# Two changes together in a two-block transformer kernel: squares summed on TensorE, and 17 weight residues prepared during block 1

## The chip, the cores and the metric

One core of one Trainium2 chip runs the whole program once. The metric is the device time of one execution in microseconds (us), the median of several runs.

## What is computed

The input x is 512 tokens by 1024 features, in fp32. It goes through two blocks, and the second takes the output of the first.

Block 1 is a mixer (chunk-band attention beside a multi-scale pooling path, joined by sigmoid gates) and a feed-forward part. In both places the result is normalised, added to x, and the sum is normalised again for the next projection:

```python
mix = (g_a * y_a + g_b * y_b) @ w_o[l]
x = x + rms_norm(mix, norm_mix_post[l])
f = conv_gated_ffn(rms_norm(x, norm_ffn_pre[l]), w_up[l], conv_w[l], conv_b[l], w_down[l])
x = x + rms_norm(f, norm_ffn_post[l])
```

Block 2 normalises x, projects it with w_in, and runs two branches on the projections: a gated delta rule (four heads, chunks of 64 tokens, a triangular solve for each chunk) and differential attention (four heads). Both results are normalised, gated and projected by w_out:

```python
hn = rms_norm_2(x, w_norm)
proj = jnp.einsum("bsd,de->bse", hn, w_in.astype(f32))
a_mat = lower + jnp.eye(c, dtype=q.dtype)
sol = lax.linalg.triangular_solve(a_mat, rhs, left_side=True, lower=True, unit_diagonal=True)
o = jnp.concatenate([o_a, o_b], axis=-1).astype(x.dtype)
return jnp.einsum("bse,ed->bsd", o, w_out)
```

## The kernel before, in words

**Layout.** Activations lie feature-major: the residual `xs` is 8 tiles of 128 features by 512 tokens. A weight piece is 128 output features by 1024 inputs (128x1024 fp32, 512 KB). `fetch` (line 371) loads pieces from DRAM on SyncE's queue into two raw buffers. `split_next` (line 382) cuts a piece into two fp32r operands: ScalarE copies it into `whi` (`split_hi`, line 350), VectorE subtracts that from the piece and writes the residue `wlo` (`split_lo`, line 356). There are four buffers of each. For every 128 inputs TensorE then does three matmuls: high by high, high by low, low by high.

**What sets the order.** The program is written out at build time by a planner, the class `Issue` (line 108). The main line issues matmuls; after each of them `step` (line 192) lets waiting generator tasks (`spawn`, line 189) issue their next instructions on the other engines, if the planner's own estimate of the engines' free times allows it. `after` (line 309) holds a task until its inputs are due, `room` (line 313) until VectorE and ScalarE have space. The order on each engine that comes out is fixed. Nearly all instructions of TensorE, VectorE, ScalarE and GpSimd come out of one helper, line 232, loads out of line 283, moves between on-chip memory and DRAM out of line 288.

**The seams.** Between a projection and the next one stands a norm, an addition and another norm. There are two such places, handled by the class `Seam` (line 518): after w_o (about 300 to 342 us) and after w_down (about 673 to 728 us). Tokens go in two halves of 256. `chain(hf)` (line 543) takes the column sums of squares of the projection's result (`rstd`, line 506: `colsum` on TensorE, one-column products `t<-ones,acc`; then a chain of 128x2 operations on VectorE, `ms`, `rsq_y`, `rsq_t`, `nc`; then `spread`, products `t<-cst,nc` that lay the factor over all partitions). For each of the 8 feature tiles it then computes on VectorE `f`, the addition into `x`, and the residue `nl`, and on ScalarE the high part `nh` and the square `sq`. GpSimd adds the squares of tiles 1 to 7 into `acc2`. After the last tile a second `rstd` on `acc2` gives the factor of the second norm, which goes into `nb` and multiplies the next projection's outputs. While this runs, TensorE does the products of the first four pieces of the next projection on each half as its tiles come out (`seam_products`, line 994: three products of 256 columns by four pieces for each tile; their tiles are `mm`, `s`, `s`, `t`). Behind the seam come units of 24 matmuls of 512 columns.

**Block 2.** Its input projection's pieces come in the order of `UNITS` (line 33). The delta rule works on two pairs of heads (`gdn_pair`, line 1165). For each pair VectorE and TensorE make the matrix L; it goes to DRAM (`dl<-L`), its diagonal blocks come back (`xt<-dl`), GpSimd solves them in about 14 us of small steps (`cb<-xt`, `xt<-xt,cb`), and the inverse goes out and comes back in its place (`dx<-xt`, `T<-dx`). TensorE then builds the full inverse (`s<-cst,T` and what follows). All these moves are on SyncE's queue, between the loads of weight pieces.

Of the kernel before, what the change touches and what calls it, by code (L numbers as in the profile page):

```python
# [17 lines left out]
P = 128  # L18
# [17 lines left out]
HEADS = [3, 0, 4, 2, 1, 5, 6, 7]  # L36
NHELD, NFIRST = 1, 6
NPART = 7
ATTN, DIFF = 6, 7
# [198 lines left out]
def kernel(ctx, tc, aps, out, dbg=None):  # L238
# [70 lines left out]
    def after(*aps):  # L309
        while iss.ready(*aps) > iss.now + LEAD:  # L310
            yield
# [49 lines left out]


    plan = weight_order()
    raws, done = [], []
# [17 lines left out]
    def split_next():  # L382
# [21 lines left out]
        else:  # L404
            off = (TOKOFF if n <= D else 0) if key[0] in tokmajor else HALFOFF if key[:2] in halves else 0
            hi = wbuf("whi", n, off)
            lo = wbuf("wlo", n, off)
            split_hi(raw, hi)
            yield
            split_lo(raw, hi, lo)  # L410
        done.append((key, hi, lo))
# [78 lines left out]

    def colsum(acc, tbs):
        ps = yield from grab("t")
        yield from after(acc[:, tbs[0] * P:(tbs[-1] + 1) * P])
        for i, tb in enumerate(tbs):
            T.matmul(ps[:, i:i + 1], acc[:, csl[tb]], ones, start=True, stop=True)
        yield
        return ps
# [20 lines left out]
    class Seam:  # L518
# [24 lines left out]
        def chain(self, hf):  # L543
# [3 lines left out]
            if hf == 0:  # L547
                self.col, self.col2, self.acc2, self.nb = tiny("nc", NT), tiny("nc", NT), act("acc"), act("nb")
            b = yield from rstd(self.acc, self.col, tbs)
            while hf and self.prog[0] < KD - 1:  # L550
                yield
            for k in range(KD + 1):
                if k < KD:
# [6 lines left out]
                    split_hi(x, self.hi[k][:, cs], pcol(self.gnext, k))  # L560
                    if k == 0:
                        A.activation(self.acc2[:, cs], x, AF.Square)
                    else:
                        sq = act("sq")
                        A.activation(sq[:, cs], x, AF.Square)
                        G.tensor_tensor(self.acc2[:, cs], self.acc2[:, cs], sq[:, cs], op=ALU.add)
                if k == KD - 1:
# [5 lines left out]
                yield from room()  # L573
            b = yield from rstd(self.acc2, self.col2, tbs)
            A.activation(self.nb[:, cs], b[:, :256], AF.Copy)
# [418 lines left out]
    def seam_products(sn, keys, finish):  # L994
# [16 lines left out]
        for hf in range(2):  # L1011
            for k in range(KD):
# [4 lines left out]
                if hf and k in (0, 4):  # L1017
# [5 lines left out]
    hhi, hlo, rb = seam_products(sn, [("w_up", i) for i, _ in units[:NS]],  # L1023
                                 lambda key, r: conv3(key[1] // 2 + key[1] % 2 * MF, r))
    for i, c in units[NS:]:
        w = weights("w_up", i)
        ps = grab_now("mm")
        gemm(ps, w, hhi, hlo)
        spawn(ffn_unit(c, ps, sn))
# [830 lines left out]
```

## Time and profile before

| | us |
|---|---|
| median of 3 runs | 1009.82 |
| lowest and highest run | 1008.95, 1013.06 |
| the profiled execution, its own time | 1010.56 |
| its span in the trace | 1008.8 |
| TensorE busy in it | 990.9 (98%) |
| VectorE busy | 682.7 (68%) |
| ScalarE busy | 497.7 (49%) |
| GpSimd busy | 83.6 (8%) |

The profiled execution's time is 1.76 us longer than its span (what lies before the first and behind the last instruction), and 0.74 us above the median. PE is TensorE's matmuls and PEld its weight loads, DVE is VectorE, ACT ScalarE, POOL GpSimd, SP SyncE; a q behind the name is that engine's DMA queue. Matmuls overlap, so the pace of TensorE is read from one start to the next and not from a single duration. One fp32 product is two instructions in the trace, one fp32r product is one.

### The profile page before, as it was taken

To read this page: it belongs to the slowest core of one execution; us is meant where nothing else is said; L and a number is where in the kernel's file an instruction comes from. 1 tells how busy PE (TensorE), PEld (TensorE's weight loads), DVE (VectorE), ACT (ScalarE), POOL (GpSimd) and SP (SyncE) were. 2 spreads that over 40 slices of the span, in tenths; PEclk is the share of its full clock that TensorE was granted. 3 is DMA by queue.
4 is the path that set the end of the run, shared out by engine and by line. 5 is a ranking of instruction groups with operands and counts; after the bars stand their busy time and mean duration, and the time that the engine had idled before them with its cause. 6 is when DMAs were issued, how large, how long until landed. Compare 5 with 4: busy or idle time off the path is not lost.

```text
span 1008.8 us, 14943 instructions
## 1 busy us (share of the span) xinstructions
PE 990.9 (98%) x5622; PEld 838.1 (83%) x5622; DVE 682.7 (68%) x1409; ACT 497.7 (49%) x1035; POOL 83.6 (8%) x162
## 2 busy tenths in 40 slices
PE   9999999999999999999999999999999998999998
PEld 7877688888898888888888888898899987888986
DVE  6587774444348997677677522259895687999973
ACT  6577533233354555344344422334456756578780
POOL 2010000000002100000001000003200261002001
PEclk9999999999999999999999999999999999999999
DMA  7422123232240132322323323230523441113322
GB/s 251 157 73 77 60 84 104 85 104 101 88 139 29 64 124 85 104 102 87 105 91 114 103 91 115 90 129 1 180 93 113 135 94 38 41 34 111 108 64 83
DMA packets 40344, 97.17 MB, mean 96 GB/s; under 512 B 12160, under 2 KB 16528, under 8 KB 40272
## 3 DMA queue, kind: packets, MB, share of 16 engines
q1 hardware_dynamic: 37392, 87.53, 26.6%
q0 software_dynamic: 2736, 8.66, 2.5%
q8 instruction: 44, 0.72, 0.3%
q14 instruction: 28, 0.23, 0.1%
q10 hardware_dynamic: 144, 0.03, 0.0%
HBM read 90.29 MB, written 5.91 MB: 95 GB/s over the span
## 4 chain that ended last, share of the span: by engine, by line
PE 82%; DVE 12%; DMA 2%; ACT 2%; issue 2%; SPq 0%; DVEq 0%; POOLq 0%; POOL 0%
PE mm L232 73%; PE t L232 6%; PE s L232 4%; DVE nl L232 2%; DVE x L232 2%; DVE wlo L232 1%; DVE f L232 1%; DVE y L232 1%; DMA w<-w_qk 1%; DVE rsq_t L232 1%; DVE acc L232 1%; DMA w<-w_a 0%; ACT whi L232 0%; DMA w<-w_v 0%; DVE r L232 0%
## 5 line engine op out<-in xcount | busy, mean ns | idle before, releaser
L232 DVE TENSOR_TENSOR wlo<-w,whi 128x1024 fp32r<-128x1024 f32 (+4 forms) x153 | 180.5, 1186 | 63.7 <-ACT whi L232 63.6
L232 PE MATMUL mm<-nh,whi 128*128 128x512 f32 x448 | 176.1, 393 | 0.3 <-DVE r L232 0.3
L232 PE MATMUL mm<-nl,whi 128*128 128x512 f32 x448 | 176.0, 393 | 0.0
L232 ACT ACTIVATE whi<-w 128x1024 fp32r<-128x1024 f32 (+4 forms) x153 | 155.0, 1018 | 42.3 <-DMA w<-w_dn 21.2
L232 PE MATMUL mm<-nh,wlo 128*128 128x512 f32 x448 | 175.8, 392 | 0.0
L232 PEld LDWEIGHTS mm<-nh,whi 128*128 128x128 f32 x448 | 84.2, 188 | 17.6 <-issue 0.7
L232 PEld LDWEIGHTS mm<-nh,wlo 128*128 128x128 f32 x448 | 84.1, 188 | 16.8
L232 PEld LDWEIGHTS mm<-nl,whi 128*128 128x128 f32 x448 | 84.2, 188 | 16.4
L232 PE MATMUL mm<-h,whi 128*128 128x512 f32 x208 | 82.4, 396 | 0.0
L232 PE MATMUL mm<-l,whi 128*128 128x512 f32 x208 | 82.1, 395 | 0.0
L232 PE MATMUL mm<-h,wlo 128*128 128x512 f32 x208 | 82.1, 395 | 0.0
L232 PE MATMUL mm<-gh,whi 128*128 128x512 f32 (+1 forms) x198 | 72.4, 366 | 0.0
L232 PE MATMUL mm<-gl,whi 128*128 128x512 f32 (+1 forms) x198 | 72.2, 365 | 0.0
L232 PE MATMUL mm<-gh,wlo 128*128 128x512 f32 (+1 forms) x198 | 72.2, 365 | 0.0
L232 ACT ACTIVATE y<-hu,par 128x512 f32<-128x512 f32 x40 | 32.4, 810 | 63.5 <-DVE hu L232 63.5
L232 DVE SCALAR_TENSOR_TENSOR y<-hu,par,y 128x511 f32<-128x511 f32 x80 | 59.9, 748 | 1.4
L232 POOL TENSOR_TENSOR acc<-acc,sq 128x256 f32<-128x256 f32 (+1 forms) x31 | 26.4, 851 | 413.8 <-ACT sq L232 413.7
L232 PE MATMUL mm<-wlo,nh 128*128 128x256 f32 (+1 forms) x192 | 54.7, 285 | 0.0
L232 PE MATMUL mm<-whi,nl 128*128 128x256 f32 (+1 forms) x192 | 54.6, 284 | 0.0
L232 DVE TENSOR_TENSOR hu<-mm,nb 128x512 f32<-128x512 f32 x40 | 27.6, 691 | 39.4 <-PE mm L232 39.4
L232 PE MATMUL mm<-whi,nh 128*128 128x256 f32 (+1 forms) x192 | 54.2, 282 | 0.0
L232 DVE TENSOR_TENSOR acc<-acc,sq 128x512 f32<-128x512 f32 (+1 forms) x21 | 14.3, 683 | 48.8 <-ACT sq L232 48.6
(352 smaller groups left out, 2166.3 us busy)
## 6 DMA issues: line engine op xcount, KB each, us to landing
w<-w_up SPq DMA_DIRECT2D x44, 512.0 KB, 3.5
w<-w_g SPq DMA_DIRECT2D x16, 512.0 KB, 3.5
w<-w_dn SPq DMA_DIRECT2D x16, 448.0 KB, 3.4
w<-w_a SPq DMA_DIRECT2D x12, 512.0 KB, 3.5
w<-w_ap SPq DMA_DIRECT2D x8, 512.0 KB, 3.5
w<-w_o SPq DMA_DIRECT2D x8, 512.0 KB, 3.4
w<-w_dn SPq DMA_DIRECT2D x8, 512.0 KB, 3.5
w<-w_z SPq DMA_DIRECT2D x8, 512.0 KB, 3.6
```

What stands on the lines that cost most here:

```text
L232: return f(*args, **kw)
```

## The change

Two edits.

**Squares.** `acc2` and its GpSimd additions are gone. ScalarE writes the squares of the 8 tiles into 8 tiles of their own (`sqs`), and `colsum` takes the list: for each block of 128 tokens it sums all 8 tiles in PSUM, 16 one-column products for each half where there were 2.

**Residues ahead.** A new task, `make_ahead`, runs during block 1's up projection, for 17 pieces of block 2: q0 (two pieces), k0 (two), k1 (two), v1 (two), the eight of z, and a11. It loads each piece in two halves of 128x512 on GpSimd's queue, ScalarE makes the high part, VectorE the residue, and GpSimd's queue stores the residue in DRAM (`low_...`). In block 2 `split_next` then loads the stored residue into `wlo` on SyncE's queue in place of VectorE's subtraction. `whi` is made as before.

```diff
@@ -35,6 +35,8 @@
 
 HEADS = [3, 0, 4, 2, 1, 5, 6, 7]
 NHELD, NFIRST = 1, 6
+
+AHEAD = ["q0", "k0", "k1", "v1"]
 NPART = 7
 ATTN, DIFF = 6, 7
 START = [("w", 0, 0), ("x", 0, 0), ("x", 1, 0), ("w", 1, 0), ("x", 2, 0), ("x", 3, 0),
@@ -360,6 +362,29 @@
             V.scalar_tensor_tensor(lo, src, scale, hi.bitcast(F32), op0=ALU.mult, op1=ALU.subtract)
 
 
+    made = {}
+
+    def make_ahead(keys):
+        for key in keys:
+            src = aps[key[0]][key[1]]
+            parts = [slice(0, 512), slice(512, src.shape[-1])]
+            low = dp.tile([P, src.shape[-1]], F32, name=f"low_{key[0]}_{key[1]}")
+            raw = [act("pr") for _ in parts]
+            for t, sl in zip(raw, parts):
+                load(nc.gpsimd, t, src[:, sl])
+            yield
+            for t, sl in zip(raw, parts):
+                hi, lo = act("prh", F32R), act("prl", F32R)
+                split_hi(t, hi)
+                yield
+                yield from room()
+                split_lo(t, hi, lo)
+                yield
+                nc.gpsimd.dma_start(low[:, sl], lo.bitcast(F32))
+            made[key] = low
+            yield from room()
+
+
     plan = weight_order()
     raws, done = [], []
     early = {("w_up", i) for i in range(NS - 1)} | {("w2_a", int(u[1:])) for u in UNITS[:NS - 1]}
@@ -405,9 +430,12 @@
             off = (TOKOFF if n <= D else 0) if key[0] in tokmajor else HALFOFF if key[:2] in halves else 0
             hi = wbuf("whi", n, off)
             lo = wbuf("wlo", n, off)
+            if key in made:
+                load(nc.sync, lo.bitcast(F32), made[key])
             split_hi(raw, hi)
             yield
-            split_lo(raw, hi, lo)
+            if key not in made:
+                split_lo(raw, hi, lo)
         done.append((key, hi, lo))
         fetch()
 
@@ -488,11 +516,14 @@
         else:
             V.tensor_tensor(t, t, r.unsqueeze(2).broadcast_to([P, NT, P]), op=ALU.mult)
 
-    def colsum(acc, tbs):
+    def colsum(accs, tbs):
+
+        accs = accs if isinstance(accs, list) else [accs]
         ps = yield from grab("t")
-        yield from after(acc[:, tbs[0] * P:(tbs[-1] + 1) * P])
+        yield from after(*(acc[:, tbs[0] * P:(tbs[-1] + 1) * P] for acc in accs))
         for i, tb in enumerate(tbs):
-            T.matmul(ps[:, i:i + 1], acc[:, csl[tb]], ones, start=True, stop=True)
+            for j, acc in enumerate(accs):
+                T.matmul(ps[:, i:i + 1], acc[:, csl[tb]], ones, start=j == 0, stop=j == len(accs) - 1)
         yield
         return ps
 
@@ -545,7 +576,7 @@
             while self.summed[hf] < KD:
                 yield
             if hf == 0:
-                self.col, self.col2, self.acc2, self.nb = tiny("nc", NT), tiny("nc", NT), act("acc"), act("nb")
+                self.col, self.col2, self.sqs, self.nb = tiny("nc", NT), tiny("nc", NT), [], act("nb")
             b = yield from rstd(self.acc, self.col, tbs)
             while hf and self.prog[0] < KD - 1:
                 yield
@@ -558,12 +589,9 @@
                     V.tensor_tensor(f, f, b[:, :256], op=ALU.mult)
                     V.tensor_tensor(x, x, f, op=ALU.add)
                     split_hi(x, self.hi[k][:, cs], pcol(self.gnext, k))
-                    if k == 0:
-                        A.activation(self.acc2[:, cs], x, AF.Square)
-                    else:
-                        sq = act("sq")
-                        A.activation(sq[:, cs], x, AF.Square)
-                        G.tensor_tensor(self.acc2[:, cs], self.acc2[:, cs], sq[:, cs], op=ALU.add)
+                    if hf == 0:
+                        self.sqs.append(act("sq"))
+                    A.activation(self.sqs[k][:, cs], x, AF.Square)
                 if k == KD - 1:
                     free(b)
                 if k > 0:
@@ -571,7 +599,7 @@
                     self.prog[hf] = k - 1
                 yield 0
                 yield from room()
-            b = yield from rstd(self.acc2, self.col2, tbs)
+            b = yield from rstd(self.sqs, self.col2, tbs)
             A.activation(self.nb[:, cs], b[:, :256], AF.Copy)
             free(b)
             self.fin[hf] = True
@@ -1022,6 +1050,7 @@
     units = [(2 * m + b, m + b * MF) for m in range(MF) for b in range(2)]
     hhi, hlo, rb = seam_products(sn, [("w_up", i) for i, _ in units[:NS]],
                                  lambda key, r: conv3(key[1] // 2 + key[1] % 2 * MF, r))
+    spawn(make_ahead([key for key in plan if key[0][3:] in AHEAD or key[0] == "w2_z" or key[:2] == ("w2_a", 11)]))
     for i, c in units[NS:]:
         w = weights("w_up", i)
         ps = grab_now("mm")
```

**TensorE, first seam, around the two column sums of its middle.** `acc` is the sum of squares of the projection's second half; `acc` in the second such row before, and `sq` in the row after, are the squares of x's first half. Before:

```order
1419 L232 MATMUL s_2829<-nh_2848,wl 128x256
1420 L232 MATMUL s_2830<-nh_2848,wh 128x256
1421 L232 MATMUL t_2902<-ones,acc 128x1 x2
1422 L232 MATMUL s_2830<-nl_2849,wh 128x256
1423 L232 MATMUL s_2830<-nh_2848,wl 128x256
1424 L232 MATMUL t_2831<-nh_2848,whi 128x256
1425 L232 MATMUL t_2831<-nl_2849,whi 128x256
1426 L232 MATMUL t_2941<-ones,acc 128x1 x2
1427 L232 MATMUL t_2831<-nh_2848,wlo 128x256
```

With the change:

```order
1419 L234 MATMUL s_2825<-nh_2844,wl 128x256
1420 L234 MATMUL s_2826<-nh_2844,wh 128x256
1421 L234 MATMUL t_2895<-ones,acc 128x1 x2
1422 L234 MATMUL s_2826<-nl_2845,wh 128x256
1423 L234 MATMUL t_2929<-ones,sq 128x1 x16
1424 L234 MATMUL s_2826<-nh_2844,wl 128x256
1425 L234 MATMUL t_2827<-nh_2844,whi 128x256
1426 L234 MATMUL t_2827<-nl_2845,whi 128x256
1427 L234 MATMUL t_2827<-nh_2844,wlo 128x256
```

The sum of x's squares comes two products earlier and has 16 products where it had 2.

**VectorE at the same place**, the two chains for the factors (`ms` reads the column sums). Before:

```order
361 L232 TENSOR_SCALAR ms<-t_2902 128x2
362 L232 TENSOR_SCALAR rsq_y<-ms 128x2
363 L232 SCALAR_TENSOR_TENSOR rsq_t<-rsq_y 128x2
364 L232 TENSOR_TENSOR rsq_t<-rsq_t,ms 128x2
365 L232 SCALAR_TENSOR_TENSOR rsq_y<-rsq_t,rsq_y 128x2
366 L232 TENSOR_SCALAR ms<-t_2941 128x2
367 L232 SCALAR_TENSOR_TENSOR rsq_t<-rsq_y 128x2
```

With the change:

```order
361 L234 TENSOR_SCALAR ms<-t_2895 128x2
362 L234 TENSOR_SCALAR ms<-t_2929 128x2
363 L234 TENSOR_SCALAR rsq_y<-ms 128x2
364 L234 SCALAR_TENSOR_TENSOR rsq_t<-rsq_y 128x2
365 L234 TENSOR_TENSOR rsq_t<-rsq_t,ms 128x2
366 L234 SCALAR_TENSOR_TENSOR rsq_y<-rsq_t,rsq_y 128x2
367 L234 TENSOR_SCALAR rsq_y<-ms 128x2
```

Both `ms` now stand ahead of both chains, so the first chain stands behind the 16 products too.

**SyncE's queue in block 2, around the solve of the delta rule** (`dl<-L` the second pair's matrix, `dx<-xt` the first pair's inverse that leaves GpSimd, `xt<-dl` the second pair's blocks for GpSimd). Before:

```order
160 L288 DMA dl<-L 128x4x128
161 L283 DMA w_7212<-w_z 128x1024
162 L288 DMA dl<-L 128x4x128
163 L288 DMA dx_4818<-xt 64x16x16
164 L283 DMA w_7257<-w_z 128x1024
165 L288 DMA xt<-dl 64x16x16
166 L288 DMA T<-dx_4818 64x8x64 x2
```

With the change:

```order
166 L290 DMA dl<-L 128x4x128 x2
167 L285 DMA wlo<-low_w_k_0_3779 128x1024
168 L290 DMA xt<-dl 64x16x16
169 L285 DMA w_7525<-w_z 128x1024
170 L285 DMA wlo<-low_w_k_1_3852 128x1024
171 L290 DMA dx_5080<-xt 64x16x16
172 L290 DMA lm<-dl 16x8x16 x4
173 L290 DMA lm<-dl 32x8x32 x2
174 L285 DMA w_7618<-w_z 128x1024
175 L290 DMA T<-dx_5080 64x8x64 x2
```

The second pair's `xt<-dl` now stands ahead of the first pair's `dx<-xt`, with a `wlo` load ahead of it; `T<-dx` stands behind one more weight load.

## Rows read from the trace of the kernel before

**Rows 1.** The page: PE's busy time; the chain that ended last, by engine.

```profile
PE 990.9 (98%) x5622; PEld 838.1 (83%) x5622; DVE 682.7 (68%) x1409; ACT 497.7 (49%) x1035; POOL 83.6 (8%) x162
PE 82%; DVE 12%; DMA 2%; ACT 2%; issue 2%; SPq 0%; DVEq 0%; POOLq 0%; POOL 0%
```

**Rows 2.** Windows by stage: start:end length, busy (x count) of PE, PEld, DVE, ACT, POOL, clock, DMA share, GB/s.

```profile
300.00:342.00 42.00, 40.10 (x301) 37.63 (x300) 35.73 (x100) 18.76 (x45) 11.02 (x14) 0.96 0.16 52
342.00:673.00 331.00, 331.00 (x1504) 275.76 (x1502) 200.21 (x266) 136.72 (x179) 3.74 (x7) 1.00 0.31 101
673.00:728.00 55.00, 52.57 (x346) 46.30 (x345) 48.03 (x115) 23.38 (x50) 15.67 (x24) 1.00 0.27 96
805.00:870.00 65.00, 58.37 (x692) 50.45 (x691) 55.34 (x129) 36.99 (x99) 22.59 (x58) 0.97 0.26 63
```

**Rows 3.** Timeline of PE in both seams (start, duration, [idle before <-releaser]); ns min/median/max of one.

```profile
318.38 0.58 PE L232 MATMUL t<-ones,acc 128*128 128x1 f32 x4 [0.98 <-DVE acc L232]
695.88 0.68 PE L232 MATMUL t<-cst,nc 128*128 128x128 f32 x4 [0.78 <-DVE nc L232]
L232 PE MATMUL t<-ones,acc x40: 168/250/271, 24.1 to 708.1; 128*128 128x1 f32 x40
```

**Rows 4.** Timeline of POOL, then of DVE, in the first seam's second half.

```profile
330.23 0.79 POOL L232 TENSOR_TENSOR acc<-acc,sq 128x256 f32<-128x256 f32 x1 [1.27 <-ACT sq L232]
331.42 0.74 POOL L232 TENSOR_TENSOR acc<-acc,sq 128x256 f32<-128x256 f32 x1 [0.40 <-ACT sq L232]
330.34 0.96 DVE L232 SCALAR_TENSOR_TENSOR nl<-x,par,nh 128x256 fp32r<-128x256 f32 x1
332.36 0.47 DVE L232 SCALAR_TENSOR_TENSOR nl<-x,par,nh 128x256 fp32r<-128x256 f32 x1
```

**Rows 5.** Timeline of the first seam's second half: DVE, PE, then DVE and PE at its end.

```profile
324.36 0.42 DVE L232 TENSOR_TENSOR f<-f,t 128x256 f32<-128x256 f32 x1 [1.65 <-PE t L232]
326.49 0.38 PE L232 MATMUL mm<-nl,wh 128*128 128x256 f32 x1 [0.27 <-DVE nl L232]
326.95 0.28 PE L232 MATMUL s<-nl,wh 128*128 128x256 f32 x1
327.07 0.28 PE L232 MATMUL s<-nh,wl 128*128 128x256 f32 x1
336.50 2.89 DVE L232 TENSOR_TENSOR wlo<-w,whi 128x1024 fp32r<-128x1024 f32 x2
341.48 0.71 PE L232 MATMUL t<-cst,nc 128*128 128x128 f32 x4
341.95 0.48 PE L232 MATMUL mm<-nh,whi 128*128 128x512 f32 x1
```

**Rows 6.** Windows: the two stretches with a lower granted clock (columns as in rows 2).

```profile
320.43:323.84 3.41, 3.41 (x19) 3.41 (x18) 1.94 (x14) 0.00 (x0) 0.00 (x0) 0.50 0.00 0
839.25:842.67 3.42, 3.40 (x37) 3.29 (x38) 0.00 (x0) 1.29 (x3) 0.00 (x0) 0.50 0.02 5
```

**Rows 7.** Timeline around the two solves: SP's queue, POOL's first step of pair 2, PE.

```profile
812.22 0.59 SPq L288 DMA_DIRECT2D dx<-xt  x1
813.62 0.59 SPq L288 DMA_DIRECT2D xt<-dl  x1
832.58 0.59 SPq L288 DMA_DIRECT2D dx<-xt  x1
818.18 1.05 POOL L232 TENSOR_TENSOR cb<-xt 64x15 f32<-64x15 f32 x1 [4.60 <-ACT dt L232]
818.86 0.32 PE L232 MATMUL s<-cst,T 64*64 64x64 f32 x2 [1.50 <-DMA T<-dx]
838.69 0.29 PE L232 MATMUL s<-cst,T 64*64 64x64 f32 x2 [3.17 <-DVE rsk L232]
```

**Rows 8.** Timeline of DVE in the up projection.

```profile
402.03 1.22 DVE L232 TENSOR_TENSOR wlo<-w,whi 128x1024 fp32r<-128x1024 f32 x1
406.20 0.69 DVE L232 TENSOR_TENSOR hu<-mm,nb 128x512 f32<-128x512 f32 x1 [1.50 <-PE mm L232]
```

## The prediction

> **What bounds the kernel now.** I read the page's busy times and the chain first, then windows by stage, then the timeline of each place where the change puts or takes something. TensorE is busy 98% of the span and holds 82% of the chain; VectorE holds 12% [rows 1]. That average hides two kinds of stage. In the up projection TensorE has no gap at all (331.00 of 331.00 us), while VectorE is busy for 200 us and ScalarE for 137 [rows 2]: there only TensorE's own work counts, and the other two engines have 131 and 194 us to give. In the two seams TensorE idles 1.90 and 2.43 us, and VectorE is busy 36 of 42 and 48 of 55 us; at 805 to 870 us TensorE idles 6.6 us [rows 2]. The change adds TensorE work in the seams and moves VectorE and queue work in block 2, so those three windows decide it.
>
> The sum is made against the profiled execution, 1010.56 us (span 1008.8). It lies 0.74 above the median of the runs, so 0.74 is taken off at the end. A measurement here can tell about 0.5% from no change: below 1004.8 counts as faster, above 1014.9 as slower.
>
> **The sums of squares, work.** One sum of squares over two token blocks takes 4 instructions and 0.58 us to its end; one of them alone lasts 0.25 us by the median, so starts lie (0.58 - 0.25) / 3 = 0.11 us apart [rows 3]. A half's sum goes from 2 products to 16, that is 14 x 2 x 0.11 = +3.1 us, and there are four such halves: **+12.3 us** of TensorE work. What of it reaches the end depends on what stood there before.
>
> *First seam, middle.* TensorE waited 0.98 us for VectorE ahead of the first sum [rows 3]. VectorE was late because GpSimd's additions of squares slow it: with an addition running (330.23 for 0.79) `nl` takes 0.96 us, without one 0.47 [rows 4]. There are 7 such additions in each half; at about 0.45 us for five to six of them a half loses some 2.5 us of VectorE. They go, so the wait goes. Behind it stood 3.41 us at a granted clock of 0.50, TensorE's level of 1.2 GHz, in which half the time, 1.7 us, was lost [rows 6]; the clock is priced apart below, so 1.7 is taken off here. Against that, VectorE's two factor chains now both stand behind the 16 products, and the first spread comes 5 products of 0.12 us later, +0.6. Together 3.1 - 1.0 - 1.7 + 0.6 = **+1.0**.
>
> *First seam, second half.* Before, from `f` at 324.36 to the product behind the last spread at 341.95 are 17.6 us [rows 5]. Six 512-column products stood ahead of the spread, which the change puts behind it; at 331 / 1504 = 0.22 us each [rows 2] that is 1.3, so 16.3 us were the seam's own. With the change: 2.1 us to the first product that needs `nl` (326.49), 95 more products at 0.12 us (326.95 to 327.07), which VectorE without GpSimd beside it can follow, 11.4; the sum, 32 x 0.11 = 3.5; the spread, 341.48 to 341.95, 0.5 [rows 5]. That is 17.5, **+1.2**. The spread stands 23 products (2.8 us) behind the sum, and VectorE's chain of eleven small operations of about 0.2 us has to fit in there, with two `wlo` subtractions (2.89 us together, rows 5 again) that stand ahead of it while the sum runs. If it doesn't fit, up to 1 us more.
>
> *Second seam.* The second half goes the same way, +1.2. In the first half no low clock was there to lose, the wait ahead of the spread was 0.78 us [rows 3], and the stretch was paced by VectorE, which gets back its 2.5: 3.1 - 0.8 - 2.5 = -0.2. **+1.0**.
>
> Seams together: 1.0 + 1.2 + 1.0 = **+3.2**. Bounds: 0, if the freed VectorE time closes every gap, to +8.0, the work less the idle time of rows 2 (12.3 - 4.3).
>
> **The clock.** Before, one of the seams' four half-ways shows the low level, right behind a wait of TensorE and a burst of one-column products [rows 3, 6]; the other such stretch, in block 2, begins behind a wait of 3.17 us [rows 7]. Now four bursts of 3.5 us, eight times as long, stand in the seams. No row shows so long a burst. I price it at 1.7 us for each burst that is followed by the low level, take two of four, half-way between the one of four before and all, **+3.4**, and keep 0 and +6.8 as the bounds. The Trainium skill ("TensorE: Matmul & The Clock Gate", Part 1) says that the gate sets the clock by how busy the array has been recently, and that the low level is the default; columns that are nearly all empty would, by that, bring the low level behind each burst, which is the second rival below. Rows 6 agree in that both stretches follow a lull, and no row shows what a burst alone does.
>
> **Up projection.** Added: 34 loads and 34 stores on GpSimd's queue, 34 ScalarE copies and 34 VectorE subtractions of 128x512. A VectorE operation of that size takes 0.69 us, and VectorE stands idle 1.50 us ahead of it in each unit [rows 8]; 34 x 0.69 = 23 us go into 131 idle ones, and on ScalarE, even at the 1.22 us of a whole piece [rows 8], 41 into 194. The DMA engines are at 0.31 [rows 2]. I cost it at **0**: the cover is that idle time, and TensorE's full window says that its operands were always there. Bounds 0 and +2: the added operation may push a `hu` or a `wlo` back by 0.69, and three such in a row would use up the 1.50. The Trainium skill ("SBUF — State Buffer", section "SBUF: two separate sides") warns that a transfer issued from GpSimd's queue can be held up while VectorE keeps the shared port; the loads would then come late and ScalarE would wait with `whi` behind it, which no row here shows.
>
> **Block 2.** Removed: 17 subtractions of 1.22 us, 20.7 us of VectorE; added: 17 loads of 512 KB on SyncE's queue. TensorE's full stages gain nothing from that. What changes is the two solves. Before, TensorE waited 1.50 us for the first pair's `T` and 3.17 for the second's, and then ran 3.42 us at the low level, losing 1.7 [rows 6, 7]. The second solve began on GpSimd at 818.18, since its `xt<-dl` (813.62) stood on the queue behind `dx<-xt` (812.22), which waits for the first solve [rows 7]. In the new order it stands ahead, so GpSimd can go on at about 813, some 5 us sooner. TensorE comes to the second `T` some 3.3 us of products sooner, and to the first some 5.4 later. So the first wait goes (-1.5), the second shrinks to 3.2 + 3.3 - 5 = about 1.2 (-2.0), and the low level behind it most likely goes (-1.7): **-5.2**. Bounds: -8.3, all 6.6 us of idle time in that window [rows 2] and the 1.7; and +4, if the new `wlo` loads hold the queue up. What is late next is the first pair's `T<-dx`, now behind one more weight load.
>
> **Sum.** 3.2 + 3.4 + 0 - 5.2 = +1.4: 1010.56 + 1.4 = 1012.0, and 0.74 less for the median, **1011.2 us**: no change that can be told.
>
> **Rivals.** *Faster:* no burst brings the low level, and all of block 2's waits go: 3.2 + 0 - 8.3 = -5.1, 1004.7 us. For it: VectorE has 20 us less to do in a stretch where it is busy 55 of 65 us [rows 2], and both waits are late VectorE, GpSimd or queue work. Against it: the order is fixed at build time, and TensorE reaches the second `T` sooner too. Chance 0.23.
>
> *The low level behind all four bursts:* 3.2 + 6.8 - 5.2 = +4.8, 1014.6, on the edge of slower, and with the seams nearer their upper bound beyond it. For it: the wait and the low level at 320.43. Against it: in the second seam two waits of the same kind brought no drop, its window has clock 1.00 [rows 2, 3]. Chance 0.20.
>
> *Slower, by SyncE's queue:* a `wlo` load has to wait until TensorE is through with the piece that held its buffer. Before, that wait stood on VectorE; now it stands on the queue, and the second pair's `xt<-dl`, then the next raw piece, stand behind it. A piece is 24 products, 24 x 0.22 = 5.3 us. If the load ahead of `xt<-dl` leaves one piece late, the second solve starts no sooner than before and the raw piece behind comes 5.3 us late: 3.2 + 3.4 - 1.5 + 5.3 = +10.4, 1020.2. It decides from the point at which that load leaves after 813.6, when `xt<-dl` left before. For it: the queue is strictly in order, and `dx<-xt` shows such a hold-up [rows 7]. Against it: there are four buffers. Chance 0.15.
>
> *No effect:* the new sums fill exactly what TensorE idled. That lies within the forecast case.
>
> **How the numbers follow.** The forecast case, about 1008 to 1014, has 0.42. Faster by over 0.5%: nearly all of the first rival, 0.23. Slower: the queue (0.15), half of the clock case (0.10) and 0.05 for seams at their upper bound, 0.30. Within: 0.47. The range takes in most of the faster rival and stops short of the queue's 1020: 1003 to 1019.
>
> **What would show it.** Right: 16-product sums of about 3.5 us each, no wait ahead of them; `nl` at 0.47 throughout the seams; units behind the first seam some 2 us later than before; no gap in TensorE during the up projection; the second solve beginning within 1 us of the first's end; 1 to 3 windows of clock 0.50 in the seams. Wrong: a burst costing other than 3.5 us, gaps in the up projection, or a `wlo` load on SyncE's queue that stands for microseconds with `xt<-dl` behind it.

## The result: about 1% slower, and the profile after

The changed kernel takes 1021.02 us (median of 4 runs, 1017.25 to 1022.21), the one before 1009.38 beside it (4 runs). The ratio is 1.0103, 95% interval 1.0083 to 1.0123: slower by 8 to 12 us, above the range of 1003 to 1019. The profiled execution took 1022.21 us, its span is 1020.2.

To see where the 11.4 us between the spans (1020.22 - 1008.79) came up, I cut both traces at the same five places: the first `t<-ones,acc` of each seam, the seventh 512-column product behind each seam (before, six of them stand ahead of the last spread; after, none), and the end of the last VectorE operation.

| stage, us | before | after | difference |
|---|---|---|---|
| to the first seam | 301.01 | 301.87 | +0.86 |
| first seam | 40.94 | 45.95 | +5.01 |
| up and down projection | 330.98 | 333.08 | +2.10 |
| second seam | 39.51 | 44.91 | +5.40 |
| block 2, to the last operation | 293.25 | 286.09 | -7.16 |
| from the last operation to the end | 3.09 | 8.31 | +5.22 |

Block 2 gained more than was forecast. Three other stages lost over 5 us each, and one of them, the end of the program, has no operation in it.

The page: PE's busy time, and the chain by engine.

```profile
PE 1002.5 (98%) x5734; PEld 854.4 (84%) x5734; DVE 674.9 (66%) x1431; ACT 515.6 (51%) x1064; POOL 95.2 (9%) x202
PE 79%; issue 7%; DVE 5%; POOL 4%; DMA 3%; ACT 1%; SPq 0%; POOLq 0%; DVEq 0%
```

TensorE is busy 1002.5 us where it was 990.9 [rows 1]. VectorE's share of the chain fell from 12% to 5%. In the chain of the first seam alone (301 to 348 us) TensorE's own work makes up 92%, where VectorE's made up 68% before (301 to 342 us): VectorE no longer paces that seam. The windows of the stages (columns as in rows 2; clock 1.00 is TensorE's level of 2.4 GHz, 0.50 its low level of 1.2 GHz):

```profile
300.00:342.00 42.00, 40.67 (x334) 40.28 (x333) 29.47 (x92) 18.84 (x45) 0.54 (x1) 0.96 0.19 65
342.00:673.00 331.00, 329.71 (x1466) 273.10 (x1465) 217.58 (x304) 151.78 (x206) 39.27 (x73) 0.99 0.47 151
673.00:728.00 55.00, 54.80 (x413) 53.94 (x412) 36.63 (x108) 23.42 (x51) 4.36 (x8) 0.91 0.28 97
805.00:870.00 65.00, 63.60 (x762) 57.49 (x762) 50.16 (x131) 41.23 (x114) 25.27 (x72) 0.97 0.44 120
```

Against [rows 2]: TensorE's idle time in the second seam's window went from 2.43 to 0.20 us, but its mean clock from 1.00 to 0.91. The up projection is no longer without a gap (329.71 of 331). In block 2's window TensorE idles 1.4 us where it idled 6.6.

**The sums of squares.** TensorE's one-column products in both seams (start, duration, instruction):

```profile
317.73 0.50 PE L234 MATMUL t<-ones,acc 128*128 128x1 f32 x4
318.30 3.81 PE L234 MATMUL t<-ones,sq 128*128 128x1 f32 x32
338.06 3.63 PE L234 MATMUL t<-ones,sq 128*128 128x1 f32 x32
696.91 3.63 PE L234 MATMUL t<-ones,sq 128*128 128x1 f32 x32
714.48 4.03 PE L234 MATMUL t<-ones,sq 128*128 128x1 f32 x32
```

There is no idle time ahead of any of them, where [rows 3] had 0.98 us. A sum of 16 products (32 instructions) takes 3.63 us; the 4.03 and 3.81 end in a stretch at the lower clock. The next fence lists all stretches with a lower granted clock up to 1010 us (in what follows, a low stretch):

```profile
321.61:325.02 3.41, 3.41 (x17) 3.41 (x18) 2.46 (x19) 0.00 (x0) 0.00 (x0) 0.50 0.02 5
342.08:345.50 3.42, 3.42 (x18) 3.42 (x17) 1.46 (x10) 0.00 (x0) 0.00 (x0) 0.50 0.26 99
700.48:703.90 3.42, 3.42 (x18) 3.42 (x17) 2.18 (x11) 0.56 (x2) 0.29 (x1) 0.50 0.00 0
717.55:724.38 6.83, 6.83 (x33) 6.83 (x34) 1.78 (x11) 0.00 (x0) 0.00 (x0) 0.50 0.16 65
840.43:843.84 3.41, 3.41 (x44) 2.84 (x43) 2.36 (x6) 1.69 (x6) 0.00 (x0) 0.50 0.44 88
```

Each of the four sums has one that begins in its last microsecond or up to 0.4 us behind its end. The last of them has twice the length. [Rows 6] had one in the seams. The four are 3.41 + 3.42 + 3.42 + 6.83 = 17.1 us at half the clock. TensorE is busy throughout them, so half of that, 8.5 us, is lost, against 1.7 before.

**VectorE in the first seam's second half**, the operations that answer to [rows 4]:

```profile
330.15 0.48 DVE L234 SCALAR_TENSOR_TENSOR nl<-x,par,nh 128x256 fp32r<-128x256 f32 x1
331.34 0.48 DVE L234 SCALAR_TENSOR_TENSOR nl<-x,par,nh 128x256 fp32r<-128x256 f32 x1
```

`nl` takes 0.48 us each time; the 0.96 beside a running GpSimd addition is gone.

**The up projection's gap**: GpSimd's queue, then ScalarE, then TensorE (with [idle before <-releaser]).

```profile
475.04 0.55 POOL L383 DMA_DIRECT2D low_w_z<-prl  x1 [4.04 <-DVE prl L234]
475.75 0.54 POOL L383 DMA_DIRECT2D low_w_z<-prl  x1 [0.16 <-issue]
476.29 1.07 POOL L285 DMA_DIRECT2D pr<-w_z  x2
480.89 0.63 ACT L234 ACTIVATE prh<-pr 128x512 fp32r<-128x512 f32 x1 [1.53 <-DMA pr<-w_z]
481.95 1.04 ACT L234 ACTIVATE whi<-w 128x1024 fp32r<-128x1024 f32 x1
483.05 0.50 PE L234 MATMUL mm<-nh,whi 128*128 128x512 f32 x1 [0.42 <-ACT whi L234]
484.64 0.50 PE L234 MATMUL mm<-nh,wlo 128*128 128x512 f32 x1 [0.86 <-DVE wlo L234]
```

ScalarE's `prh` waits 1.53 us for its load. The load was issued at 476.29, behind two stores on the same queue, the first of which had waited 4.04 us for VectorE. ScalarE works in order, so `whi` of the next piece is late behind it, TensorE waits 0.42 us for `whi` and 0.86 for the `wlo` made from it.

**Block 2**, SyncE's queue, GpSimd's last step of the first solve and first step of the second, and TensorE's largest wait for them:

```profile
813.73 1.61 SPq L290 DMA_DIRECT2D dl<-L  x2
815.47 0.47 SPq L285 DMA_DIRECT2D wlo<-low_w_k  x1
818.03 0.59 SPq L290 DMA_DIRECT2D xt<-dl  x1
821.87 0.61 SPq L290 DMA_DIRECT2D dx<-xt  x1
821.60 0.24 POOL L234 TENSOR_TENSOR xt<-xt,cb 64x15 f32<-64x15 f32 x1
823.17 0.28 POOL L234 TENSOR_TENSOR cb<-xt 64x15 f32<-64x15 f32 x1
838.34 0.77 PE L234 MATMUL s<-D,lm 64*64 64x64 f32 x16 [1.28 <-POOL xt L234]
```

The `wlo` load leaves right behind the two stores `dl<-L`, without a wait of its own. The second pair's `xt<-dl` leaves at 818.03, 0.08 us after the second of these stores has landed (817.95), so it waits for the blocks that it reads and not for the `wlo` load. It still leaves before `dx<-xt` (821.87), so the second solve begins 1.3 us behind the first one's last step (821.60 + 0.24 to 823.17), where it began 6 us behind it. Both solves took 26.7 us from first to last step (811.45 to 838.19), before 34.3 (798.25 to 832.55); the first alone took 10.4 us, before 13.9. TensorE has no wait for `T` any more; of the 1.50 and 3.17 of [rows 7] one of 1.28 for `xt` is left.

**The end.** VectorE's last operation:

```profile
1011.48 0.42 DVE L234 TENSOR_TENSOR xr<-mm,xr 128x256 f32<-128x256 f32 x1 [0.59 <-PE mm L234]
```

It ends at 1011.90, and the span goes on to 1020.2. In the trace's records of the sequencers the last thing that goes on then is a DRAIN instruction of GpSimd: 9.21 us, from 1010.24 to 1019.45. Before, it took 3.91 us, from 1004.03 to 1007.93, and ended with SyncE's wait for the last store (1007.97).

### The profile page after: what moved, and what is told of

Its sections match the earlier page's. It is cut to its first block, busy times and chain, and to the rows that moved or that the text cites. A ratio compares the mean times of both kernels' runs of the same rounds, so it can differ in the third digit from the quotient of the medians.

```text
span 1020.2 us, 15357 instructions
## 1 busy us (share of the span) xinstructions
PE 1002.5 (98%) x5734; PEld 854.4 (84%) x5734; DVE 674.9 (66%) x1431; ACT 515.6 (51%) x1064; POOL 95.2 (9%) x202
## 4 chain that ended last, share of the span: by engine, by line
PE 79%; issue 7%; DVE 5%; POOL 4%; DMA 3%; ACT 1%; SPq 0%; POOLq 0%; DVEq 0%
PE mm L234 64%; PE t L234 9%; PE s L234 7%; DMA pr<-w_z 1%; DVE wlo L234 1%; POOL pr L285 1%; DVE y L234 1%; POOL xt L234 1%; POOL low_w_z L383 1%; POOL cb L234 1%; DMA w<-w_qk 1%; DVE prl L234 0%; DMA w<-w_v 0%; DVE hu L234 0%; DMA xt<-dl 0%
## 5 line engine op out<-in xcount | busy, mean ns | idle before, releaser
L234 DVE TENSOR_TENSOR wlo<-w,whi 128x1024 fp32r<-128x1024 f32 (+4 forms) x136 | 158.6, 1173 | 59.9 <-ACT whi L234 59.5
L234 PEld LDWEIGHTS mm<-h,whi 128*128 128x128 f32 x208 | 39.1, 188 | 8.5 <-issue 0.9
L234 PEld LDWEIGHTS mm<-l,whi 128*128 128x128 f32 x208 | 39.1, 188 | 8.4 <-issue 1.2
```

Of the source, the lines that this page charges most:

```text
L234: return f(*args, **kw)
```

## The experiments

Theory after the result: the loss has three sources that don't depend on each other. Bursts of one-column products bring the low clock (seams); the transfers on GpSimd's queue make its last drain long (end) and come late (up projection); against that, the residues made ahead shorten block 2. The rivals are named with each run. The same cuts for the kernels that were run (profiled executions; the first column is the time to the first seam):

| us | start | seam 1 | projections | seam 2 | block 2 | end | span |
|---|---|---|---|---|---|---|---|
| before | 301.01 | 40.94 | 330.98 | 39.51 | 293.25 | 3.09 | 1008.8 |
| the change | 301.87 | 45.95 | 333.08 | 44.91 | 286.09 | 8.31 | 1020.2 |
| seams_only | 300.81 | 45.95 | 330.86 | 44.90 | 292.34 | 3.08 | 1017.9 |
| ahead_only | 301.09 | 39.40 | 334.78 | 39.50 | 287.13 | 8.32 | 1010.2 |
| ahead_sp | 300.72 | 39.41 | 330.98 | 39.50 | 286.82 | 3.01 | 1000.4 |
| after_sp | 301.07 | 47.54 | 330.85 | 44.94 | 289.57 | 3.30 | 1017.3 |
| spaced_sp | 300.88 | 41.16 | 330.85 | 40.17 | 288.16 | 3.33 | 1004.5 |
| pool68a | 300.96 | 39.80 | 330.98 | 39.48 | 292.62 | 8.31 | 1012.2 |

The row of before holds two low stretches, one in its first seam and one in block 2, with 1.7 us lost in each [rows 6]. The profiled runs of ahead_only and ahead_sp hold none and pool68a's only one in block 2, so in the first seam, and for ahead_only and ahead_sp in block 2, up to 1.7 us of their distance to before is the clock and not the edit.

### seams_only: the sums alone

```diff
-    spawn(make_ahead([key for key in plan if key[0][3:] in AHEAD or key[0] == "w2_z" or key[:2] == ("w2_a", 11)]))
```

> Only the seams' edit; no residues made ahead. Theory: the change's loss in the seams is its own (about +10 us from the start of the first seam's sums to the units behind the second, of which some 6.8 are stretches at a granted clock of 0.50 behind the 16-product sums), and what the change lost at the start (0.86 us) and after the last operation (8.3 us from the last VectorE operation to the end, where it was 3.1) belongs to the other edit. So about +10 us, ratio near 1.010, stretches of clock 0.50 behind all four sums, the end 3.1 us behind the last VectorE operation, block 2's waits as before. Rival: the end is late because the seams' edit moves GpSimd's work; then the end comes some 8 us behind the last operation here too. Rival on the clock: the low level follows waits, not sums; then fewer than four stretches where no wait stands ahead.

Measured: 1018.66 us (5 runs), ratio 1.0059, interval 1.0039 to 1.0078. The seams take 45.95 and 44.90 us, to 0.01 what they take in the change; the end is as before. The clock (windows around the stretches):

```profile
320.00:324.20 4.20, 4.20 (x24) 4.20 (x24) 2.81 (x21) 0.00 (x0) 0.00 (x0) 0.59 0.02 4
341.20:344.60 3.40, 3.40 (x18) 3.40 (x18) 1.29 (x9) 0.00 (x0) 0.00 (x0) 0.50 0.15 55
696.20:703.00 6.80, 6.80 (x34) 6.80 (x34) 3.58 (x17) 1.62 (x4) 1.12 (x2) 0.50 0.10 38
716.70:720.10 3.40, 3.40 (x18) 3.40 (x17) 1.55 (x10) 0.00 (x0) 0.00 (x0) 0.50 0.06 24
```

All four sums are followed by the low level (the first window is wider than its stretch), this time with the double one behind the third. So the seams' loss is the seams' own, and the end is not. The ratio is smaller than expected: the profiled span is 9.1 us longer, but other runs of it show a higher mean clock (0.991 and 0.992 in the two quickest, 0.988 in the profiled one). That fits a loss that varies with how many low stretches a run has.

### ahead_only: the residues alone, by GpSimd's queue

```diff
-                    if hf == 0:
-                        self.sqs.append(act("sq"))
-                    A.activation(self.sqs[k][:, cs], x, AF.Square)
+                    if k == 0:
+                        A.activation(self.acc2[:, cs], x, AF.Square)
+                    else:
+                        sq = act("sq")
+                        A.activation(sq[:, cs], x, AF.Square)
+                        G.tensor_tensor(self.acc2[:, cs], self.acc2[:, cs], sq[:, cs], op=ALU.add)
```

(Cut, against the changed kernel: it puts the seams of the kernel before back and keeps `make_ahead`.)

> Only the residues made ahead, by GpSimd's queue as in the change; seams as before. Theory: start +0.9, up projection +2, block 2 -7, end +5: about +1 us, ratio near 1.001, with GpSimd's last drain at about 9 us where it was 3.9. Rival: block 2's gain in the change came from the changed instruction order behind the other seams, not from the residues; then there is no gain here and the ratio is near 1.008.

Measured: 1010.21 us (10 runs), ratio 0.9997, interval 0.9981 to 1.0013. Block 2 gains 6.1 us, the end loses 5.2, the projections 3.8. TensorE has three waits in the projections, 2.1 us together:

```profile
487.27 0.50 PE L234 MATMUL mm<-nh,whi 128*128 128x512 f32 x1 [0.37 <-ACT whi L234]
488.87 0.50 PE L234 MATMUL mm<-nh,wlo 128*128 128x512 f32 x1 [0.86 <-DVE wlo L234]
501.14 0.50 PE L234 MATMUL mm<-nh,wlo 128*128 128x512 f32 x1 [0.85 <-DVE wlo L234]
```

Set beside ahead_sp, which has the same 1500 products in this stage, product by product, all of the 3.8 us comes up between 472 and 503 us, at these waits and in the products next to them, which are further apart too. The start is as before (+0.08): the 0.86 us of the change don't belong to this edit, and the starts of all kernels in the table lie between 300.72 and 301.87. Most of block 2's gain belongs to the residues: the second solve begins 1.3 us behind the first one's last step here too (811.05 to 812.36), while in seams_only it begins 6.3 us behind it (821.53 to 827.84), as before. The rival doesn't fall entirely. TensorE's waits in block 2 add up to 8.2 us before, 4.3 here and 2.5 in the change, but to 6.0 in seams_only, where the one of 3.17 us for `rsk` [rows 7] is gone. So some 2 us of what the change saves there came with the seams alone in that run. This edit by itself costs as much as it brings.

### ahead_sp: the same transfers on SyncE's queue

```diff
-                load(nc.gpsimd, t, src[:, sl])
+                load(nc.sync, t, src[:, sl])
-                nc.gpsimd.dma_start(low[:, sl], lo.bitcast(F32))
+                yield from after(lo)
+                nc.sync.dma_start(low[:, sl], lo.bitcast(F32))
```

(On top of ahead_only's edit.)

> As ahead_only, but the 34 loads and 34 stores go by SyncE's queue, the stores issued once the planner holds them to be made. Theory (the number of transfers on GpSimd's queue sets the length of its last drain and the delay at the start): drain 3.9 us and start as before, so -7 +2 = about -5 us, ratio 0.995. Rival (the added work as such, instructions or semaphores, makes the end long): drain near 9 us and ratio as ahead_only. Risk: the loads on SyncE's queue hold up w_up's pieces; then TensorE shows gaps in the up projection of several us.

Measured: 1005.17 us (4 runs), ratio 0.9932, interval 0.9914 to 0.9951. The up and down projections and block 2's window:

```profile
342.00:671.00 329.00, 329.00 (x1493) 274.16 (x1493) 219.55 (x300) 154.09 (x211) 3.72 (x7) 1.00 0.49 155
805.00:870.00 65.00, 62.04 (x765) 55.18 (x763) 52.34 (x138) 41.28 (x121) 18.90 (x50) 1.00 0.32 95
```

No gap in the first (329.00 of 329.00), and the last drain is 3.90 us again. The work is the same, 34 copies, 34 subtractions, 68 transfers of the same bytes. Two things differ, the queue and `after(lo)`, which holds each store back until the planner counts its data as made. For the drain the pool runs below settle that the queue's transfers are the cause; which of the two takes the waits out of the up projection was not run apart. The risk did not come true. Of the 8.4 us between the spans (1008.8 and 1000.4) 3.4 are the two low stretches that this run lacks; the four timed runs are 5.5 us under before by their median, about as expected, and their mean clocks (0.997 to 1.000, before 0.993 to 0.998) say that part of this too is the clock.

### bursts: one-column products where nothing waits

```diff
+    bursts = {4: 16, 8: 16, 12: 16, 16: 8, 20: 8, 24: 8, 28: 4, 32: 4, 36: 32}
+        if u in bursts:
+            pb = grab_now("t")
+            for j in range(bursts[u]):
+                T.matmul(pb[:, :1], xs[j % KD][:, :P], ones, start=True, stop=True)
+            free(pb)
```

(Cut: `u` counts the units of the up projection.)

> The kernel before with bursts of one-column fp32 products put between units of the up projection, where TensorE has no gap at all: 16, 16, 16, 8, 8, 8, 4, 4 and 32 products. Theory: a burst brings the 1.2 GHz level by itself; a stretch of clock 0.50 of 3.4 us behind each burst of 16 (3.5 us) and at least one behind 32, none behind 4; 8 is open. Time +24.6 us for 112 products at 0.22, and 1.7 per stretch: +31 us. Rival: the low level needs a wait ahead; then clock 1.00 throughout and +25 us.

Measured in one run: span 1041.2, +32.4 us. The first two bursts on TensorE, neither with a wait ahead (the first row shows 25 of its burst's 32 instructions, the last of which starts at 365.54):

```profile
361.50 2.89 PE L232 MATMUL t<-ones,x 128*128 128x1 f32 x25
390.06 3.63 PE L232 MATMUL t<-ones,x 128*128 128x1 f32 x32
```

And windows behind the first, at and behind the second, at the third burst of 16, the first of 8, the first of 4, and at the burst of 32:

```profile
364.20:371.03 6.83, 6.83 (x22) 5.67 (x22) 4.82 (x7) 3.97 (x5) 0.00 (x0) 0.50 0.26 80
390.06:393.69 3.63, 3.63 (x34) 3.63 (x33) 2.36 (x3) 1.76 (x2) 0.00 (x0) 1.00 0.01 3
394.90:398.31 3.41, 3.41 (x10) 2.63 (x9) 1.39 (x2) 2.07 (x3) 0.00 (x0) 0.50 0.53 159
417.04:424.00 6.96, 6.96 (x48) 6.35 (x47) 4.23 (x6) 3.26 (x5) 0.00 (x0) 1.00 0.26 84
442.43:446.00 3.57, 3.57 (x25) 3.25 (x24) 2.45 (x4) 1.76 (x2) 0.00 (x0) 1.00 0.02 7
513.25:517.00 3.75, 3.75 (x22) 3.22 (x21) 2.63 (x4) 2.11 (x3) 0.00 (x0) 1.00 0.01 5
562.10:572.34 10.24, 10.24 (x42) 9.56 (x43) 2.56 (x4) 2.21 (x3) 3.71 (x7) 0.50 0.40 104
```

The first burst of 16 runs at 0.50 from 2.7 us after its start, for 6.83 us; the second is followed by 3.41 us at 0.50, 1.2 us behind its end; the third by none, and none of 8 or 4 by any. The burst of 32 runs at 0.50 from 3.4 us after its start, for 10.24 us. So a burst as long as the change's sums brings the low level by itself, two times in three here, and the rival falls: no wait is needed. The change's sums did it four times in four, those of seams_only and after_sp too.

### after_sp: the whole change on SyncE's queue

The edit of ahead_sp, made to the changed kernel.

> The whole change, but make_ahead's loads and stores on SyncE's queue. Theory: what ahead_sp gained over ahead_only (5.3 us of GpSimd's last drain and 2 us of gaps in the up projection) comes here too: some 6 us under the change, ratio to before near 1.004, with four or five stretches of clock 0.50 in the seams left. Rival: the two edits work on each other (the residues' gain in block 2 needs the old seams); then more than that stays.

Measured: 1017.92 us (4 runs), ratio 1.0078, interval 1.0056 to 1.0100: 3 us under the change where 6 were expected. The end and the projections are as before the change; the seams are not. The stages fit the sum of the single edits but for two. The first seam is 1.6 us longer than in the change: its second sum brought 6.8 us at the low level where the change had 3.4. Block 2 gained 3.7 us where ahead_sp gained 6.4; a low stretch of 6.8 us stands there, where ahead_sp has none. Both fit the clock. TensorE's waits in block 2 are 4.5 us here and 4.2 in ahead_sp, so the 2 us that the new seams save there alone do not come on top with this queue; I see no other sign that the edits work on each other.

### spaced_sp: the same products, not in bursts

```diff
+            p2 = yield from grab("t")
             for k in range(KD + 1):
+                if k > 0:
+                    sq = self.sqs[k - 1]
+                    yield from after(sq[:, cs])
+                    for i, tb in enumerate(tbs):
+                        T.matmul(p2[:, i:i + 1], sq[:, csl[tb]], ones, start=k == 1 and i == 0, stop=k == KD and i == 1)
...
-            b = yield from rstd(self.sqs, self.col2, tbs)
+            b = yield from rstd(None, self.col2, tbs, p2)
```

(On top of after_sp's edit, cut: `rstd` takes the finished sums `p2`.)

> As after_sp, but a half's 16 products are spread over the half: two for each feature tile as its square is made, one accumulation group. Theory: the bursts bring the low level, so without bursts no stretch of clock 0.50 in the seams (about 17 us at half clock in the change: -8.5), against some +3 us for 32 more changes between fp32 and fp32r products; the sum's latency behind the last tile falls from 3.5 to 0.4 us. About 5 us under after_sp, ratio near 0.999. Rival: the low level comes from the number of one-column products in a stretch, however they are spread; then as many stretches as in after_sp and a time above it.

Measured: 1006.56 us (10 runs), ratio 0.9957, interval 0.9938 to 0.9976: 11 us under after_sp. The seams' windows:

```profile
300.00:342.00 42.00, 42.00 (x355) 41.78 (x355) 32.58 (x103) 20.63 (x47) 0.00 (x0) 1.00 0.21 73
673.00:713.00 40.00, 39.83 (x335) 39.42 (x334) 31.25 (x99) 17.77 (x40) 4.37 (x8) 1.00 0.29 106
```

Clock 1.00, and TensorE idles 0.0 and 0.2 us. The seams take 41.16 and 40.17 us, 11.2 less together than in after_sp with the same 16 products for each half. The rival falls: it is the burst, not the number of products. The gain is larger than the 5 us expected, since after_sp lost 10.2 us to the clock in the seams (20.5 us of stretches), not 8.5. Still the seams are no faster than ahead_sp's with GpSimd's additions (39.41 and 39.50). In these runs the TensorE sums bring nothing even without the clock.

### pool68, pool68r, pool68a, pool34a: what the last drain counts

```diff
+        for j in range(2 if u < 34 else 0):
+            load(nc.gpsimd, extra[(2 * u + j) % 4][:128, :8], aps["rel"][0][:128, :8])
```

(Cut: `u` counts units, `extra` is four new tiles of 128x8. pool68r: `[:8, :8]`. pool68a and pool34a: into `act("ex")[:, :8]` in place of four new tiles, two and one for each unit.)

> The kernel before with 68 small loads more on GpSimd's queue (128 rows of 32 bytes each), two in each unit of the up projection, read by nobody. Theory: the last drain grows with the number of transfers on that queue, (9.21 - 3.91) / 68 = 0.078 us for each; so 9.2 us here, and the end 5.3 us later. Rival: it grows with the bytes (17.8 MB in the change, 0.3 MB here); then 3.9 to 4.0 us.

> As pool68, but 8 rows of 32 bytes for each transfer. By the number of transfers: 9.2 us again. By the number of rows: about 3.91 + 5.3 / 16 = 4.2 us.

> The kernel before with 68 loads of 128 rows of 32 bytes on GpSimd's queue, into tiles of the activation pool that nobody reads, so that no tile is added to the layout (pool68 had four tiles more, and its 512-column products ran 232 ns apart in place of 227). Theory: cadence 227, drain 9.2 us, the end 5.3 us later and nothing else: ratio 1.005. Rival: the loads themselves slow the products; then 232 ns again and about +17 us.

> As pool68a with 34 loads. If the drain grows in step with the number of transfers: 3.91 + 34 x 0.078 = 6.56 us. Rival: a step (a queue that has been round once); then 3.9 or 9.2.

GpSimd's last drain, from the sequencers' records, beside the transfers issued on its queue in the whole program:

```
kernel       transfers   drain us
before          37         3.91
seams_only      37         3.90
ahead_sp        37         3.90
pool34a         71         6.44
the change     105         9.21
ahead_only     105         9.21
pool68         105         9.21
pool68r        105         9.21
pool68a        105         9.21
```

Transfers of 256 KB, of 128 rows of 32 bytes, and of 8 rows give the same 9.21 us; 34 give half of it: (6.44 - 3.91) / 34 = 0.074 and (9.21 - 6.44) / 34 = 0.081 us for each. So the number of transfers counts, not bytes or rows; in the change the 68 were done at 502 us, 508 us before the drain began. What the drain does in that time the trace doesn't say. pool68a, timed: 1014.45 us (4 runs), ratio 1.0044, interval 1.0031 to 1.0057, which holds the +5.2 us of its end; no other stage of it lost.

pool68 and pool68r themselves (one run each, like pool34a) became 17 us longer, not 5. Their 512-column products ran 232 ns apart, start to start, where all other kernels so far had 227, so their times are not read here.

### tiles_only: four tiles of 32 bytes a row

```diff
+    extra = [small(f"ex{j}", 8) for j in range(4)]
+    for t in extra:
+        V.memset(t, 0.0)
```

> The kernel before with pool68's four tiles of 128x8 and no transfers (each set to zero once on VectorE). If the tiles' place in the layout made pool68's products slow: 232 ns between 512-column products and some +12 us, drain 3.9. If not: 227 and no change.

Measured in one run: span 1019.9, 232 ns between 512-column products, drain 3.92. So four small tiles, without any transfer, slow every 512-column product by 2%; products of 256 columns are 118 ns apart in the up and down projection with and without them. That they do it through the place of the other tiles in memory is the nearest reading, but no address was looked at.

### ahead_sp2: the fastest version once more

> ahead_sp once more, with more rounds, as the candidate for the fastest version: ratio 0.993 again (0.991 to 0.995), drain 3.9 us, no gap in the up projection.

Measured: 1004.19 us (6 runs), ratio 0.9941, interval 0.9927 to 0.9955. The stages are those of ahead_sp within 0.6 us. Half of the change, on another queue, is 0.6% quicker than the kernel before, and by that quicker than the change too.

## Why the prediction was wrong

Two steps made most of the miss: the sum had no term for the end of the program (+5.2 us), and it took a low stretch behind two of the four sums where all four had one (5.1 us too little). Step by step:

- **The sums, work**: right. 16 products take 3.63 us where 3.5 was worked out, no wait stands ahead of them, and `nl` is at 0.48. Seams without the clock: +10.4 us (5.01 + 5.40) less 8.5 is +1.9 against +3.2.
- **The clock**: right in mechanism, mis-sized. "Take two of four, +3.4": all four brought the low level, one of them twice as long, 8.5 us. The rival with all four, 6.8, was nearer and had a chance of 0.20. Its step that failed is the middle between one of four before and all; the one of before stood behind bursts of 0.6 us and told nothing of bursts of 3.6. The Trainium skill ("TensorE: Matmul & The Clock Gate", Part 1) says that the clock follows how busy the array has been. That sentence alone doesn't tell the outcome: in the second burst of bursts TensorE shows as busy for 3.63 of 3.63 us, and the low level followed. The rival that the prediction drew from it, the low level behind each burst, was borne out.
- **The up projection**, "I cost it at 0", bounds to +2: measured +2.1 in the change and +3.8 in ahead_only, around TensorE's waits for weights; in the change they go back to a late load of `pr`. I counted the engines' idle time as cover, and not that the loads stand behind stores on the same queue, which wait for VectorE, and that a late load holds up `whi` on ScalarE. On SyncE's queue, with the stores held back, the stage costs 0. The hold-up that the Trainium skill ("SBUF — State Buffer", section "SBUF: two separate sides") warns of was not seen: the loads of z landed 4.5 us after issue (median) by GpSimd's queue and 4.1 by SyncE's, those of k 4.2 and 4.5. The load behind the waits at 483 us was 4.6 us under way (476.29 to 480.87), about the median: it was late because it was issued late.
- **The end**: missing from the sum, +5.2 us, the largest single error. The prediction counted the 68 transfers only where they run and has no term for what lies behind the last operation. The runs show a price for each transfer on GpSimd's queue, 0.078 us, paid at the end. Nothing covers it: before, the drain ended together with the last store (1007.93 and 1007.97), so transfers added show from the first on; pool34a's 34 made the end 2.5 us longer.
- **Block 2**: -7.2 against -5.2. The steps of the two waits were right: the first went, the second solve began on the heels of the first, and of the second wait 1.28 us are left where 1.2 was worked out. The third step failed: the low level behind the second wait, 1.7 us, did not go in the profiled run, a stretch stands at 840.43. So the steps that came true were worth 3.5 us, and 3.7 more came than was added up. GpSimd's solves themselves became shorter (10.4 us the first, before 13.9), and some 2 us of TensorE's waits went with the seams alone, as seams_only shows; the rest is not broken down.
- **Rival, SyncE's queue**: the `wlo` load ahead of `xt<-dl` did not hold it up. It left at 815.47, and `xt<-dl` at 818.03, when `dl<-L` had landed. Nor did that wait cost anything, since GpSimd was at the first solve until 821.84.

The stages give +5.01 + 2.10 + 5.40 - 7.16 + 5.22 + 0.86 = +11.4 and the forecast had +1.4. Of the 10 us between, 5.2 are the end, 5.1 the clock, 2.1 the up projection and 0.9 the start, less 1.3 in the seams' work and 2.0 in block 2. The start's 0.86 was seen in no other kernel of the table. It comes up at 24.97 us, in one wait of TensorE for VectorE (1.46 us), before any instruction that the change touches, and is left as scatter.

What stays open: the ratios of the single edits (1.0059 and 0.9997) multiply to 1.0056, 4.7 us less than the change's 1.0103, though the profiled spans nearly add up (+9.1 and +1.4, against +11.4). 1.3 of the 4.7 us is the kernel before itself, whose median was 1009.38 beside the change and 1010.71 beside the single edits. The number of low stretches differs between runs of one kernel and may make up the rest, which is not shown: the records of the runs without a profile hold only a mean clock.

## What to carry to other kernels

Before work is moved to an idle engine's queue, ask what that queue costs besides time on it: here each transfer on GpSimd's queue added about 0.078 us to the end of the program, whatever its size, and the same transfers on SyncE's queue added nothing there. Narrow products on TensorE should be spread among wide ones: 16 of one column in one go brought the low clock in 14 of 15 cases, and two at a time did not. When two edits come together, run each alone first: here one was worth -6 us in one place and the other +10 in another.

## What the runs showed of the hardware that was not expected

- GpSimd's DRAIN at the end: 3.91, 6.44 and 9.21 us for 37, 71 and 105 transfers on its queue.
- A burst of one-column products with no wait on either side: low clock behind two of three bursts of 3.6 us, behind none of 1.8 or 0.95, and a stretch of 10.24 us with the one of 32 products, 7 us long at 0.11 us for each of its 64 instructions.
- Four tiles of 32 bytes a row that nobody reads: 232 in place of 227 ns between 512-column products, +11 us in span (one run; two more with the same tiles show 232 as well).
